# Moving a rotary kernel's later loads and its stores from SyncE's DMA queue to GpSimd's, one packet per engine

## The chip, the cores and the metric

The kernel runs on one core of one Trainium2 chip. The time is device microseconds (us) of one execution; lower is better. Of the core's engines it uses VectorE (DVE) for all arithmetic, and SyncE (SP) and GpSimd (POOL) only to issue transfers, which 16 DMA engines carry out.

## The reference

The input `x` has shape (16, 512, 16, 64): batch, sequence, heads, dimension, in float32, 33.55 MB. `cos` and `sin` have shape (512, 32). Half of each head's 64 values is rotated by a table that depends on the place in the sequence, and the other half is copied through.

```python
x1, x2 = (x[..., :half_dim].copy(), x[..., half_dim:].copy())
rotated_first = x1[..., :half_dim // 2] * cos[..., :half_dim // 2] - x1[..., half_dim // 2:] * sin[..., :half_dim // 2]
rotated_second = x1[..., :half_dim // 2] * sin[..., :half_dim // 2] + x1[..., half_dim // 2:] * cos[..., :half_dim // 2]
return np.concatenate([rotated_first, rotated_second, x2], axis=-1).astype(np.float32)
```

So 33.55 MB must be read and as many written, for about three operations on each value of one half.

## The kernel before

The 8192 rows (batch times sequence) are cut into `T` = 4 tiles. A tile has 128 partitions of `K` = 16 rows, 64 KB in each partition, 8.39 MB in all. On-chip memory holds three of them, the `ring` with `NS` = 3 slots: tile t lies in slot t mod 3, so that tile 3 is loaded over tile 0, once tile 0 has been stored. A tile is rotated in place and then stored whole, the half that is copied through included.

- **Table.** L63 and L64 bring in `cos` and `sin` on POOL's queue (64 KB each), and DVE spreads them over the partitions (L73 to L86).
- **First loads.** L65 to L67 issue on SP's queue the loads of tile 0, of tile 1, and of the first half (`KC` = 8 of 16 rows) of tile 2. None of them waits for anything.
- **Rotation.** `rotate(t, lo, hi)` (L90) is four DVE operations: two products (L96, L97), a difference (L98) and a sum (L101). Each tile takes two calls of half a tile, tile 2 three: rows 0 to 8, 8 to `KM` = 13, and 13 to 16.
- **Behind it on SP's queue**, in this order: the store of tile 0, the load of the second half of tile 2 (which waits for nothing), the load of tile 3 (which waits until the store of tile 0 has landed), the store of tile 1, the store of tile 3.
- **On POOL's queue**: the store of tile 2 (L116), so that it stands in another queue than the store of tile 1.
- **One order by hand**: L118 to L123 make the store of tile 1 wait for `near`, the end of rotating rows 8 to 13 of tile 2, although tile 1 has been ready for longer; the reason given is that it should come behind the loads at the DMA engines.

An engine issues its transfers in program order, and one that waits holds up those behind it on the same engine. Each transfer of 128 partitions is shared by all 16 DMA engines, 8 partitions for each.

Of the kernel before, what the change touches and what calls it, by code (L numbers as in the profile page):

```python
# [1 line left out]

# [4 lines left out]


@with_exitstack
def kernel(  # L10
    ctx: ExitStack,
    tc: tile.TileContext,
    x: bass.AP,
    cos: bass.AP,
    sin: bass.AP,
    out: bass.AP,
):
    nc = tc.nc
    fp32 = mybir.dt.float32
    P = 128  # L20
    B, S, H, D = x.shape
    Q = D // 4
    HF = D // 2

    K = 16
    T = B * S // (P * K)
    PB = S // K
    REP = P // PB  # L30
    R = H * D
    NS = 3
    KC = K // 2
    KM = 13

    xf = x.rearrange("b s h d -> (b s h d)").rearrange("(t p f) -> t p f", t=T, p=P)
    of = out.rearrange("b s h d -> (b s h d)").rearrange("(t p f) -> t p f", t=T, p=P)
    cosf = cos.rearrange("(p k) j -> p (k j)", k=K)
    sinf = sin.rearrange("(p k) j -> p (k j)", k=K)

    const_pool = ctx.enter_context(tc.tile_pool(name="const", bufs=1))
    b_pool = ctx.enter_context(tc.tile_pool(name="bp", bufs=1, space=bass.MemoryType.PSUM))


    ring = const_pool.tile([P, NS, K, H, D], fp32)
    stage = const_pool.tile([P, 2, K, HF], fp32)
    spun = const_pool.tile([P, 2 * K, Q], fp32)
    packed = const_pool.tile([PB, 2 * K, Q], fp32)
    table = const_pool.tile([P, 2, K, 2, Q], fp32)

    def rows(t, lo, hi):
        return ring[:, t % NS, lo:hi].rearrange("p k h d -> p (k h d)")

    def load(t, lo=0, hi=K):
        return nc.sync.dma_start(out=rows(t, lo, hi), in_=xf[t, :, lo * R : hi * R])

    def store(t, lo=0, hi=K, queue=nc.sync):
        return queue.dma_start(out=of[t, :, lo * R : hi * R], in_=rows(t, lo, hi))  # L58


    nc.vector.memset(stage[:, :, :, 0:Q], 0.0)  # L61
    spread = stage.rearrange("(j b) t k i -> j b t (k i)", b=REP)
    nc.gpsimd.dma_start(out=spread[:, 0, 0], in_=cosf)  # L63
    nc.gpsimd.dma_start(out=spread[:, 0, 1], in_=sinf)  # L64
    load(0)  # L65
    load(1)
    load(2, 0, KC)  # L67

    PQ = PB // REP
    nc.vector.stream_shuffle(  # L73
        out=spun[:],
        in_=stage.rearrange("p t k j -> p (t k) j")[:, :, 0:Q],
        mask=[j % PQ * REP for j in range(PB)],
    )
    for q in reversed(range(REP)):
        n = PQ * (q + 1)
        nc.vector.tensor_copy(out=packed[0:n], in_=spun[q * PB : q * PB + n])  # L80

    for r in range(REP):
        nc.vector.tensor_copy(  # L83
            out=table[r * PB : (r + 1) * PB].rearrange("p t k c j -> p (t k) c j"),
            in_=packed.unsqueeze(2).to_broadcast((PB, 2 * K, 2, Q)),
        )  # L86
    C = table[:, 0].rearrange("p k c j -> p k (c j)")
    Sn = table[:, 1].rearrange("p k c j -> p k (c j)")

    def rotate(t, lo, hi):  # L90
        x1 = ring[:, t % NS, lo:hi, :, 0:HF]
        c = C[:, lo:hi].unsqueeze(2).to_broadcast((P, hi - lo, H, HF))
        s = Sn[:, lo:hi].unsqueeze(2).to_broadcast((P, hi - lo, H, HF))
        b_full = b_pool.tile([P, KC, H, HF], fp32, name="b_t")
        b_t = b_full[:, 0 : hi - lo]
        nc.vector.tensor_mul(out=b_t, in0=x1, in1=s)  # L96
        nc.vector.tensor_mul(out=x1, in0=x1, in1=c)  # L97
        nc.vector.tensor_sub(  # L98
            out=x1[:, :, :, 0:Q], in0=x1[:, :, :, 0:Q], in1=b_t[:, :, :, Q:HF]
        )  # L100
        return nc.vector.tensor_add(  # L101
            out=x1[:, :, :, Q:HF], in0=x1[:, :, :, Q:HF], in1=b_t[:, :, :, 0:Q]
        )

    rotate(0, 0, KC)
    rotate(0, KC, K)
    store(0)
    load(2, KC, K)
    load(3)
    rotate(1, 0, KC)  # L110
    rotate(1, KC, K)
    behind_loads = store(1)
    rotate(2, 0, KC)
    near = rotate(2, KC, KM)
    rotate(2, KM, K)
    store(2, queue=nc.gpsimd)  # L116

    tc.add_manual_dep(  # L118
        behind_loads.ins,
        near.ins.name,  # L120
        mybir.DependencyInfo(mybir.DependencyClass.Sync, mybir.DependencyReason.DATA),
        reason="the store follows the loads at the DMA engines",
    )  # L123
    rotate(3, 0, KC)
    rotate(3, KC, K)
    store(3)


# [1 line left out]
_INS = ['x', 'cos', 'sin']  # L130
_OUTS = [((16, 512, 16, 64), 'float32')]


# [23 lines left out]
```

## Time and profile before

| What | Value |
|---|---|
| median of 3 runs | 161.5 us (161.34 to 161.62) |
| span of the profiled execution, first to last instruction | 159.5 us |
| the median less that span (start and end around it) | 2.0 us |
| DVE busy | 112.9 us, its last operation ends at 131.2 us |
| POOL busy | 1.9 us |
| bytes moved | 67.24 MB, 422 GB/s over the span |
| on SP's queue (`q1 hardware_dynamic`) | 58.72 MB in 1152 packets |
| on POOL's queue (`q0 software_dynamic`) | 8.52 MB in 208 packets |

Packets are what the DMA engines are seen to carry out, one after the other. A transfer of a whole tile shows as 128 packets of 64 KB, 8 for each of the 16 engines, and 16 tiny ones that report its end. Transfers are listed with the time from issue to landing, which is when the last of those 16 reports has arrived. When the transfers of a tile are issued and land, from the issues and the times to landing in narrow windows (us from the span's start):

| Transfer | Issued by | Issued | Landed |
|---|---|---|---|
| load, tile 0 | SP | 0.74 | 22.9 |
| load, tile 1 | SP | by 1.3 | 42 |
| load, tile 2, first half | SP | by 1.7 | 52 |
| store, tile 0 | SP | 49.87 | 71.8 |
| load, tile 2, second half | SP | 50.26 | 81.4 |
| load, tile 3 | SP | 71.8 | 100.7 |
| store, tile 1 | SP | 98.86 | 132.1 |
| store, tile 2 | POOL | 104.58 | 144.1 |
| store, tile 3 | SP | 131.2 | 158.6 |

In a table of windows, the bytes and the busy time of a packet are counted where it begins. In a short window the DMA share can so be above 1 or be nothing, though the engines run without a break. In such a table the columns are: window in us, its length, busy us of DVE and of POOL with their instructions, PE clock, DMA share, GB/s.

### The profile page before, as it was taken

To read this page: it belongs to the slowest core of one execution; us is meant where nothing else is said; L and a number is where in the kernel's file an instruction comes from. 1 tells how busy PE (TensorE), PEld (TensorE's weight loads), DVE (VectorE), ACT (ScalarE), POOL (GpSimd) and SP (SyncE) were. 2 spreads that over 40 slices of the span, in tenths; PEclk is the share of its full clock that TensorE was granted. 3 is DMA by queue.
4 is the path that set the end of the run, shared out by engine and by line. 5 is a ranking of instruction groups with operands and counts; after the bars stand their busy time and mean duration, and the time that the engine had idled before them with its cause. 6 is when DMAs were issued, how large, how long until landed. Compare 5 with 4: busy or idle time off the path is not lost.

```text
span 159.5 us, 115 instructions
## 1 busy us (share of the span) xinstructions
DVE 112.9 (71%) x47; POOL 1.9 (1%) x7
## 2 busy tenths in 40 slices
DVE  1000959999999999999999999999999990000000
POOL 3000000000000000000000000010000000000000
DMA  7969979899699699699996996996996996998966
GB/s 263 542 263 542 444 345 526 362 427 526 271 493 551 263 526 526 263 395 427 493 526 263 526 526 263 526 526 263 526 526 263 526 510 279 526 427 362 526 263 263
DMA packets 1360, 67.24 MB, mean 422 GB/s; under 512 B 176, under 2 KB 176, under 8 KB 208
## 3 DMA queue, kind: packets, MB, share of 16 engines
q1 hardware_dynamic: 1152, 58.72, 85.7%
q0 software_dynamic: 208, 8.52, 12.4%
HBM read 33.69 MB, written 33.55 MB: 422 GB/s over the span
## 4 chain that ended last, share of the span: by engine, by line
DVE 61%; DMA 14%; issue 5%; DVEq 1%
DVE b_t L96 22%; DVE ring L97 22%; DMA ring<-in_x_dram 14%; DVE ring L101 10%; DVE ring L98 7%; DVEq L152 1%; DVEq L96 0%
## 5 line engine op out<-in xcount | busy, mean ns | idle before, releaser
L96 DVE TENSOR_TENSOR b_t<-ring,table 128x4096 f32<-128x4096 f32 (+2 forms) x9 | 35.6, 3959 | 2.1 <-DMA ring<-in_x_dram 1.9
L97 DVE TENSOR_TENSOR ring<-ring,table 128x4096 f32<-128x4096 f32 (+2 forms) x9 | 35.6, 3950 | 0.3
L98 DVE TENSOR_TENSOR ring<-ring,b_t 128x2048 f32<-128x2048 f32 (+2 forms) x9 | 18.4, 2050 | 0.3
L101 DVE TENSOR_TENSOR ring<-ring,b_t 128x2048 f32<-128x2048 f32 (+2 forms) x9 | 18.4, 2043 | 0.0
L73 DVE LOAD_MASK_SELECT spun<-stage x1 | 0.0, 14 | 14.4 <-DMA stage<-in_sin_dram 14.4
L83 DVE COPY table<-packed 32x1024 f32<-32x1024 f32 x4 | 2.7, 684 | 0.1
L58 POOL DMA_DIRECT2D out_dram<-ring x1 | 0.6, 559 | 101.7 <-DVE ring L101 101.7
L80 DVE COPY packed<-spun 32x512 f32<-32x512 f32 (+3 forms) x4 | 1.7, 416 | 0.1
L61 DVE MEMSET stage<- 128x512 f32 x1 | 0.5, 485 | 0.9 <-PEq L141 0.9
L73 DVE STREAM_SHUFFLE spun<-stage 128x512 f32<-128x512 f32 x1 | 0.7, 722 | 0.0
L63 POOL DMA_DIRECT2D stage<-in_cos_dram x1 | 0.6, 642 | 1.3 <-DVE stage L61 1.3
L64 POOL DMA_DIRECT2D stage<-in_sin_dram x1 | 0.5, 532 | 0.0
L141 POOL MEMSET const-bfloat16-1.0<- 128x1 bf16 x1 | 0.1, 101 | 0.0
L141 POOL MEMSET const-float32-0.0<- 128x1 f32 x1 | 0.1, 98 | 0.2 <-issue 0.2
L141 POOL MEMSET const-float32-1.0<- 128x1 f32 x1 | 0.1, 98 | 0.0
L141 POOL MEMSET const-uint8-127<- 128x1 uint8 x1 | 0.1, 98 | 0.0
## 6 DMA issues: line engine op xcount, KB each, us to landing
ring<-in_x_dram SPq DMA_DIRECT2D x2, 4096.0 KB, 40.7
stage<-in_cos_dram POOLq DMA_DIRECT2D x1, 64.0 KB, 8.9
stage<-in_sin_dram POOLq DMA_DIRECT2D x1, 64.0 KB, 13.3
ring<-in_x_dram SPq DMA_DIRECT2D x3, 28.9
out_dram<-ring SPq DMA_DIRECT2D x3, 27.4
out_dram<-ring POOLq DMA_DIRECT2D x1, 39.5
```

The source lines that it names most:

```text
L58: return queue.dma_start(out=of[t, :, lo * R : hi * R], in_=rows(t, lo, hi))
L61: nc.vector.memset(stage[:, :, :, 0:Q], 0.0)
L63: nc.gpsimd.dma_start(out=spread[:, 0, 0], in_=cosf)
L64: nc.gpsimd.dma_start(out=spread[:, 0, 1], in_=sinf)
L73: nc.vector.stream_shuffle(out=spun[:], in_=stage.rearrange("p t k j -> p (t k) j")[:, :, 0:Q], mask=[j % PQ * REP for j in range(PB)],)
L80: nc.vector.tensor_copy(out=packed[0:n], in_=spun[q * PB : q * PB + n])
L83: nc.vector.tensor_copy(out=table[r * PB : (r + 1) * PB].rearrange("p t k c j -> p (t k) c j"), in_=packed.unsqueeze(2).to_broadcast((PB, ...
L96: nc.vector.tensor_mul(out=b_t, in0=x1, in1=s)
L97: nc.vector.tensor_mul(out=x1, in0=x1, in1=c)
L98: nc.vector.tensor_sub(out=x1[:, :, :, 0:Q], in0=x1[:, :, :, 0:Q], in1=b_t[:, :, :, Q:HF])
L101: return nc.vector.tensor_add(out=x1[:, :, :, Q:HF], in0=x1[:, :, :, Q:HF], in1=b_t[:, :, :, 0:Q])
L152: with _tile.TileContext(nc) as tc:
```

## The change

```diff
-    def store(t, lo=0, hi=K, queue=nc.sync):
-        return queue.dma_start(out=of[t, :, lo * R : hi * R], in_=rows(t, lo, hi))
+    def reload(t, lo=0, hi=K):
+        return nc.gpsimd.dma_start(
+            out=rows(t, lo, hi), in_=xf[t, :, lo * R : hi * R], single_packet=True
+        )
+
+    def store(t, lo=0, hi=K):
+        return nc.gpsimd.dma_start(
+            out=of[t, :, lo * R : hi * R], in_=rows(t, lo, hi), single_packet=True
+        )
...
-    store(0)
-    load(2, KC, K)
-    load(3)
+    front = store(0)
+    second = reload(2, KC, K)
+    tc.add_manual_dep(
+        second.ins,
+        front.ins.name,
+        mybir.DependencyInfo(mybir.DependencyClass.NoSync, mybir.DependencyReason.DATA),
+        reason="the queue keeps the order of the program",
+    )
+    reload(3)
...
-    store(2, queue=nc.gpsimd)
+    store(2)
```

- The first three loads stay on SP's queue, and `cos` and `sin` on POOL's, as they were.
- The six transfers behind them (store of tile 0, load of the second half of tile 2, load of tile 3, stores of tiles 1, 2 and 3) are all issued by POOL, in this order. SP issues nothing after the first three loads.
- Each of the six is asked for as a single packet: what one DMA engine carries of it (8 rows of 64 KB, or of 32 KB for half a tile) is to be one packet where it was 8.
- The added dependency keeps the load of tile 2's second half behind the store of tile 0 in POOL's program; it is an order, not a wait.
- The waits stay: the load of tile 3 for the landing of tile 0's store, the store of tile 1 for `near`, the stores of tiles 0, 2 and 3 for their last rotation and their load. They are now POOL's.
- DVE's operations and their order are the same.

## The prediction

> **What bounds the kernel now.** I read the totals first, then the transfers with their windows, then what DVE waits for.
>
> ```profile
> span 159.5 us, 115 instructions
> DVE 112.9 (71%) x47; POOL 1.9 (1%) x7
> ...
> HBM read 33.69 MB, written 33.55 MB: 422 GB/s over the span
> ```
>
> DVE, the busiest engine, works 71% of the span and has ended at 131.2 us. The last 28 us are transfers alone. So the question is whether the 16 DMA engines ever rest. In this table of windows, watch how many bytes begin in windows of 0.6 us:
>
> ```profile
> 1.70:2.30 0.60, 0.00 (x0) 0.60 (x1) 1.00 5.30 1748
> 49.80:50.40 0.60, 0.56 (x2) 0.00 (x0) 1.00 2.02 874
> 50.40:51.00 0.60, 0.60 (x1) 0.00 (x0) 1.00 0.00 0
> 51.00:51.60 0.60, 0.60 (x1) 0.00 (x0) 1.00 4.05 1748
> 51.60:53.40 1.80, 1.80 (x1) 0.00 (x0) 1.00 0.00 0
> 53.40:54.00 0.60, 0.60 (x1) 0.00 (x0) 1.00 4.03 1748
> 67.90:68.50 0.60, 0.60 (x1) 0.00 (x0) 1.00 4.62 1748
> ...
> 97.40:98.00 0.60, 0.60 (x2) 0.00 (x0) 1.00 4.03 1748
> 99.80:100.40 0.60, 0.60 (x1) 0.00 (x0) 1.00 4.05 1748
> ```
>
> 1748 GB/s times 0.6 us is 1.05 MB: one packet of 64 KB for each of the 16 engines. The share times the window is its mean time, 4.03 x 0.60 = 2.418 us. The packets begin at 51.0 to 51.6, and the next ones 2.4 us later: back to back. 2.418 us for 64 KB is 27.1 GB/s for an engine and 434 GB/s for 16. One tile is 8 such packets, 19.3 us, and the eight tile transfers (four loads, four stores) are 154.8 us of the 159.5. The rest is 1.7 us before the first packet, a slow first packet (5.30 x 0.60 = 3.18, so 0.76 over), 0.35 where a store is followed by a load (67.9: 4.62 x 0.60 = 2.77), the packets of `cos` and `sin`, and about a microsecond behind the last landing. The kernel is bound by the DMA engines, and the change can only add gaps between packets, or take something off a packet.
>
> **The change part by part.** The span and the 2.0 us around it give the 161.5 us of the median, so what the span gains or loses is added to 161.5.
>
> *The handover at 51 us.* The store of tile 0 is issued when DVE ends its last rotation at 49.85 (L101, 47.57 and 2.28 long). The second row of the table is the last packet of SP's first three loads, 2.02 x 0.60 = 1.21 us long, so the engines run dry between 51.0 and 51.6. The store's packets begin in just that window: SP was in time, with nothing to spare that can be seen. POOL is slower in two steps that the timeline shows:
>
> ```profile
> 0.74 1.33 SPq L55 DMA_DIRECT2D ring<-in_x_dram  x3
> 49.87 0.35 SPq L58 DMA_DIRECT2D out_dram<-ring  x1
> ...
> 103.33 0.95 DVE L101 TENSOR_TENSOR ring<-ring,b_t 128x768 f32<-128x768 f32 x1
> 104.58 0.56 POOL L58 DMA_DIRECT2D out_dram<-ring  x1 [101.70 <-DVE ring L101]
> ```
>
> SP issues 0.02 us behind the DVE operation that it waits for (49.87), and takes 0.35. POOL starts 0.30 behind it (104.58 against 103.33 + 0.95) and takes 0.56. So POOL has the store of tile 0 issued at 49.85 + 0.30 + 0.56 = 50.71, where SP had it at 50.22.
>
> What comes between POOL's issue and the first packet the trace doesn't show, since both times POOL issued here the engines were busy with SP's packets. For SP it can be read: the first load is issued from 0.74 for 0.33 to 0.43 us and its first packets begin from 1.7 on, some 0.6 us after the issue. The lower bound for POOL is nothing; the upper is the tile 2 store, issued at 105.14, whose packets begin at 109.5, 4.4 us later, mostly spent behind SP's packets. Nearest is SP's row. POOL's issue is 1.6 times SP's, so I take 1.6 x 0.6 = 0.95 us. First packets then begin at 51.66, 0.66 us behind 51.0, with the spread that they have now. **Gap: 0.66 us** (0 to 4.1).
>
> The first packet after a rest may be long, as the first of all was: 0.76 over, after 1.7 us without a packet. In proportion to the gap, 0.66 / 1.7 x 0.76 = **0.3 us** (0 to 0.76).
>
> The Trainium skill speaks against the change here: "DMA: Bandwidth & Descriptors", in "Issuing engine by pattern", gives simple loads and stores to SyncE, and its table of specifications puts the first byte at about 1 us on GpSimd's path and 0.6 on SyncE's. By that, as an estimate, POOL's packets would begin at 50.71 + 1.0 = 51.7 or, counted as 0.4 us more than SP's 0.6, at the same 51.7: a gap of 0.7 us. No row here shows POOL's part by itself.
>
> *The second handover, at 100 us.* The store of tile 1 waits for `near`, which ends at 98.83. Its issue on POOL ends at 98.83 + 0.86 = 99.69 and its packets can begin at 100.64. The last packets of tile 3's load begin at 97.4 to 98.0 and end 2.42 later, at 99.8 to 100.4. With SP there was no gap. By itself POOL would leave one of 0.8, but the gap at 51 us moves everything behind it by 0.96, so that the load now ends at 100.8 to 101.4: **nothing is added**. The lateness is paid once, at the first handover.
>
> *The other four.* The second half of tile 2 is issued by POOL right behind the store of tile 0, 19 us before its turn. The load of tile 3 waits for that store to land (71.8, then 72.8), and its issue is covered by tile 2's half, which keeps the engines for 9.7 us. Behind that wait stand the stores of tiles 1, 2 and 3, on POOL now; the first of them is due at 98.8. The stores of tiles 2 and 3 are issued at 105.1 and about 132, while the engines are busy with tiles 1 and 2 until some 139. **Nothing.** If the store of tile 1 were late, all behind it would be, one for one.
>
> *DVE.* It waits for the second half of tile 2 at 90.2 (landed at 81.4) and for tile 3 at 104.3 (landed at 100.7), so that 0.96 later costs it nothing; from 3.6 on, tile 3's rotation would move, and the store behind it has 8 us of cover more. SP, with nothing left to issue, takes no work off the bound.
>
> *One packet where there were eight.* The rows of 64 KB and 32 KB give what a packet costs beyond its bytes: twice 2.02 x 0.60, less 4.03 x 0.60, is 0.006 us. Six transfers lose 7 borders each, 42 x 0.006 = **0.25 us gained** (0 to 0.6 within the rounding of the shares). The row at 67.9, where a store meets a load, could give another 0.35, or stay; I leave it. The skill's same page ("Why small descriptors are slow (HBM only)") puts a fixed cost of some 3 cycles on a packet and holds joining them worthwhile only up to 256 B. By that the gain is no more than the row's, and the packets are 256 times too long for it; as the row is the measurement, it stands.
>
> **Sum:** 161.5 + 0.66 + 0.3 - 0.25 = **162.2 us**.
>
> **The rivals.**
>
> *No gap (faster).* One mechanism: POOL's descriptors reach the engines before 51.0, within 0.3 us of its issue. Then the packets follow each other as now, and the saved borders remain: 161.5 - 0.25 = 161.25, down to 160.9 with all of the borders (0.6), or 160.55 with the 0.35 at the store-to-load border as well. For it: SP's store was in time with no gap to be seen, and POOL's issue ends only 0.49 later. Against: 0.3 us is half of what SP needs. It decides below a gap of 0.25.
>
> *A long start.* 2 to 4.4 us from POOL's issue to the first packet: a gap of 1.7 to 4.1, and up to 0.76 on the packet, 163 to 166.1. For it: `cos`, issued at 2.34, has its packets only at 7.2. Against: these, like those of the tile 2 store, waited behind packets of 64 KB.
>
> *Long packets run worse.* If each single packet starts up as the first load did, 6 x 0.76 = 4.6 us are lost, 166. For it: no packet above 64 KB is in this trace. Against: packets of the tile 2 store, on POOL's queue, take 2.42 as SP's do.
>
> *The change doesn't do what it says:* packets stay 64 KB. Then 161.5 + 0.96 = 162.5.
>
> **How the numbers follow.** Forecast 0.45, no gap 0.35, packets unchanged 0.07, long start 0.08, long packets 0.05. The predicted time is the forecast's 162.2; its own range is 161.6 to 163.0. About 0.2%, 0.3 us, is what a measurement of this kernel can tell from no change. Of "no gap", 0.28 is faster by more than that and 0.07 within it; of the forecast 0.05 is within it and 0.40 slower; unchanged packets give 0.02 and 0.05; the last two are slower. Faster 0.28, same 0.14, slower 0.58. The range goes from 160.9 (no gap, most of the borders saved) to 163.6 (a start of 2 us and a slow first packet); the longer starts, the long packets and the very best case are left out.
>
> **What would show it.** The windows around 51 us show the steps: the first packets of the tile 0 store should begin at 51.6 to 52.3, on POOL's queue, and take more than 2.42 us per 64 KB. At 100 us the packets of tile 1's store should follow the load without a gap. POOL's queue should show some 16 large packets for a tile, with fewer in all. The prediction is wrong if the packets at 51 us leave no gap, if one opens at 100 us as well, or if a tile takes more than 19.4 us in mid-stream.

## The result and the profile after

The changed kernel takes 162.47 us (median of 6 runs, 162.26 to 162.84) where the kernel before takes 161.53 in the same runs: a ratio of 1.0059, 95% interval 1.0049 to 1.0069. It is slower by 0.9 us. The profiled execution has a span of 160.3 us, 0.8 more than before. These are the page's lines on the span, the busy engines and the queues:

```profile
span 160.3 us, 115 instructions
## 1 busy us (share of the span) xinstructions
DVE 112.9 (70%) x47; POOL 4.6 (3%) x12
...
DMA packets 1360, 67.24 MB, mean 419 GB/s; under 512 B 176, under 2 KB 176, under 8 KB 208
## 3 DMA queue, kind: packets, MB, share of 16 engines
q0 software_dynamic: 928, 46.27, 67.3%
q1 hardware_dynamic: 432, 20.97, 30.6%
```

DVE is busy as long as before. POOL's queue now carries 46.27 MB. There are 1360 packets, as many as before: a transfer on POOL's queue still shows as packets of 64 KB or 32 KB.

The windows around the first handover, in the changed kernel (columns as before):

```profile
49.70:50.40 0.70, 0.67 (x2) 0.27 (x1) 1.00 1.73 749
50.40:51.20 0.80, 0.80 (x1) 0.80 (x2) 1.00 0.00 0
51.20:51.60 0.40, 0.40 (x1) 0.01 (x1) 1.00 7.43 2622
...
97.90:98.50 0.60, 0.60 (x1) 0.00 (x0) 1.00 4.03 1748
100.30:100.91 0.61, 0.58 (x2) 0.00 (x0) 1.00 3.98 1719
```

SP's last load packets begin at 49.7 to 50.4 and take 1.21 us, to 51.0 to 51.6. All 16 first packets of the tile 0 store begin between 51.2 and 51.6 (2622 GB/s x 0.40 us is 1.05 MB). So there is hardly a gap, at most 0.3 us on the engines that were done first and next to nothing on the last. But these packets take 7.43 x 0.40 = 2.97 us where 2.42 is usual: **0.55 us over**. They are not long alike. The four that begin last come right behind the load's last packets (which begin at 50.26 to 50.32 and take 1.21), without a rest:

```profile
51.40:51.60 0.20, 0.20 (x1) 0.00 (x0) 1.00 4.30 1311
```

These take 4.30 x 0.20 x 16/4 = 3.44 us, 1.0 over. The other twelve, most of them after a short rest, are 0.4 over in the mean.

At 100 us the store of tile 1 follows the load of tile 3 without a gap and at full pace (3.98 x 0.61 = 2.43).

The issues on POOL, from its timeline:

```profile
50.13 0.56 POOL L63 DMA_DIRECT2D out_dram<-ring  x1 [47.24 <-DVE ring L108]
50.68 0.53 POOL L58 DMA_DIRECT2D ring<-in_x_dram  x1
72.62 0.53 POOL L58 DMA_DIRECT2D ring<-in_x_dram  x1 [21.40 <-DMA out_dram<-ring]
99.10 0.54 POOL L63 DMA_DIRECT2D out_dram<-ring  x1 [25.96 <-DVE ring L108]
104.55 0.54 POOL L63 DMA_DIRECT2D out_dram<-ring  x1 [4.91 <-DVE ring L108]
131.44 0.53 POOL L63 DMA_DIRECT2D out_dram<-ring  x1 [26.35 <-DVE ring L108]
```

The load of tile 3 lands 28.7 us after its issue, at 101.3, against 100.7 before; the last store lands 27.8 us after its issue, at 159.2, against 158.6. So 0.6 us are lost before 101 us, and nothing from there to the last landing. From it to the end of the span are 1.1 us, where before there were 0.9. That is where the 0.8 went: 0.6 at the handover, and 0.2 behind the last landing.

### The profile page after: what moved, and what is told of

Its sections match the earlier page's. It is cut to its first block, busy times and chain, and to the rows that moved or that the text cites. A ratio compares the mean times of both kernels' runs of the same rounds, so it can differ in the third digit from the quotient of the medians.

```text
span 160.3 us, 115 instructions
## 1 busy us (share of the span) xinstructions
DVE 112.9 (70%) x47; POOL 4.6 (3%) x12
## 2 busy tenths in 40 slices
DMA packets 1360, 67.24 MB, mean 419 GB/s; under 512 B 176, under 2 KB 176, under 8 KB 208
## 3 DMA queue, kind: packets, MB, share of 16 engines
q0 software_dynamic: 928, 46.27, 67.3%
## 4 chain that ended last, share of the span: by engine, by line
issue 51%; DVE 15%; DMA 14%; POOL 2%; POOLq 0%; DVEq 0%
DMA ring<-in_x_dram 14%; DVE b_t L103 6%; DVE ring L104 6%; DVE ring L108 3%; DVE ring L105 1%; POOL out_dram L63 1%; POOL ring L58 1%; POOLq L165 0%; POOLq L63 0%; DVEq L103 0%
## 5 line engine op out<-in xcount | busy, mean ns | idle before, releaser
L63 POOL DMA_DIRECT2D out_dram<-ring x4 | 2.2, 541 | 104.5 <-DVE ring L108 104.5
L58 POOL DMA_DIRECT2D ring<-in_x_dram x2 | 1.1, 530 | 21.4 <-DMA out_dram<-ring 21.4
## 6 DMA issues: line engine op xcount, KB each, us to landing
ring<-in_x_dram POOLq DMA_DIRECT2D x1, 28.7
```

Source lines behind the costliest of these rows:

```text
L58: return nc.gpsimd.dma_start(out=rows(t, lo, hi), in_=xf[t, :, lo * R : hi * R], single_packet=True)
L63: return nc.gpsimd.dma_start(out=of[t, :, lo * R : hi * R], in_=rows(t, lo, hi), single_packet=True)
```

## The experiments

Each was timed in turns with the kernel before on one chip; ratios are to that. "Lost" is worked out as above: the mean time of the 16 packets that begin in a window (share x window, x 16 over the packets in it where they are fewer) less 2.42 us, or 1.51 for rows of 40 KB.

**1. The flag.** The changed kernel without `single_packet`, and the kernel before with it on POOL's one store:

```diff
-            out=..., in_=..., single_packet=True
+            out=..., in_=...
```

> The changed kernel without single_packet, all else as changed. Theory (POOL's later start is paid at the handover at 51 us, about 0.6 us, and some 0.2 us come behind the last landing; the flag does nothing): 162.4 us, first packets of the tile 0 store about 3.0 us long as with the flag. Rival (the flag makes the loss, since one long packet starts slowly): 161.5 to 161.7, first packets at 2.42. If the flag saves packet borders as I predicted (0.25): 162.7.

Measured: 162.87 us, 1.0072 (1.0059 to 1.0085), which overlaps the change's interval. Two lines of its profile, which is of the slowest of the five runs (163.47):

```profile
51.40:52.00 0.60, 0.60 (x1) 0.04 (x1) 1.00 4.42 1748
q0 software_dynamic: 928, 46.27, 66.9%
```

The first packets begin at 51.4 to 52.0, a little later than with the flag, and take 4.42 x 0.60 = 2.65. Without the flag nothing is won back, so it doesn't make the loss. The times alone would allow a flag that saves the predicted 0.25, since 162.87 is nearer to the 162.7 which that gives than to 162.4. The packets speak against it: 928 on POOL's queue with the flag and without, so it joined none.

```diff
-    store(2, queue=nc.gpsimd)
+    nc.gpsimd.dma_start(out=of[2], in_=rows(2, 0, K), single_packet=True)
```

> The kernel before with single_packet on the one store that POOL issues (tile 2's), which runs beside tile 1's on SP's queue and there takes turns with it, 64 KB each, and lands 39.5 us after its issue. If the flag makes one packet of what an engine carries: no turns, tile 2's store runs in one piece of 19.3 us and lands some 25 to 30 us after its issue, and tile 1's store later instead. If it does nothing: turns as before, 39.5. Time 161.55 either way.

Measured: 161.58 us, 1.0008 (0.9996 to 1.0019). The store with the flag lands after the same time as before, by the list of issues:

```profile
out_dram<-ring POOLq DMA_DIRECT2D x1, 39.5
```

It still takes turns with tile 1's store. For rows of 64 KB the flag changes nothing that these runs can see.

**2. Only the stores of tiles 1, 2 and 3 on POOL.**

```diff
-    front = store(0)
-    second = reload(2, KC, K)
...
-    reload(3)
+    store_sp(0)
+    load(2, KC, K)
+    load(3)
```

> Store of tile 0, second half of tile 2 and load of tile 3 back on SP's queue as before; the stores of tiles 1, 2 and 3 stay on POOL. Theory with the lateness paid once, at whichever handover comes first: the packets at 51 us as before (2.42 us, no loss), and now a loss of 0.4 to 0.7 us at 100 us, where POOL's issue of tile 1's store ends at 99.6 and the load before it runs out at 99.9 to 100.4; 162.1 to 162.5. Rival (only the handover at 51 us costs): 161.7. Rival (each of the six transfers on POOL costs a like share, 0.15): 161.95, with no loss at 100 us.

Measured: 162.36 us, 1.0049 (1.0037 to 1.0061). (`store_sp` is the old `store` on SP's queue.) The loss has moved from 51 to 100 us, as "paid at the first handover" has it, and the time lies in its 162.1 to 162.5, above both rivals:

```profile
51.00:51.90 0.90, 0.90 (x1) 0.00 (x0) 1.00 2.70 1165
...
97.60:98.10 0.50, 0.50 (x2) 0.00 (x0) 1.00 4.84 2097
98.10:100.50 2.40, 2.37 (x2) 0.56 (x1) 1.00 0.00 0
100.50:100.70 0.20, 0.20 (x1) 0.00 (x0) 1.00 12.69 5243
```

At 51 us, on SP's queue alone, the store's packets take 2.70 x 0.90 = 2.43. At 100 us the load's last packets end at 100.0 to 100.5, POOL's begin at 100.5 to 100.7 and take 12.69 x 0.20 = 2.54: a gap of about 0.3 and 0.12 over. Here POOL really comes late, and what is lost is mostly the gap.

**3. The lateness covered, by more rows ahead.** 10 of tile 2's rows in SP's first load, so that its packets last 2.4 us longer; then also tile 1's store released one row earlier:

```diff
-    load(2, 0, KC)
+    load(2, 0, 10)
...
-    second = reload(2, KC, K)
+    second = reload(2, 10, K)
```

> The changed kernel, with 10 of tile 2's 16 rows in SP's first load instead of 8, so that SP's packets run out 2.4 us later, at 53.4 to 54.0, and POOL's store of tile 0 is waiting by then. Theory (paid once): nothing lost at 51 to 54 us, and 0.4 to 0.7 lost at 100 us, 162.1 to 162.5. Rival (only the first handover costs): 161.7. Rival (a like share for each transfer): 162.4, with no loss at either place.

> As the run with 10 rows ahead, and the store of tile 1 waits for row 12 of tile 2 instead of row 13, so that POOL issues it some 1.7 us earlier, at about 97.4. Both handovers are covered. Theory: no loss at 51 to 54 us and none at 100 us; only what comes behind the last landing is left, 161.6 to 161.8. Rival (a like share for each transfer on POOL): 162.4.

Measured: 162.57 us, 1.0064 (1.0049 to 1.0080), and with `KM = 12` 162.47 us, 1.0058 (1.0046 to 1.0070). The theory's 161.6 to 161.8 for the second fell. The 162.4 of a like share for each transfer is near both times, but experiment 2 spoke against it (161.95 forecast, 162.36 measured), and here too the loss stands in one place. With 10 rows ahead the loss at the first handover is not gone; here the windows of the first of the two runs:

```profile
49.00:49.50 0.50, 0.50 (x1) 0.00 (x0) 1.00 3.03 1311
50.50:51.00 0.50, 0.50 (x1) 0.50 (x2) 1.00 3.78 1311
52.30:53.00 0.70, 0.70 (x1) 0.00 (x0) 1.00 3.05 936
```

SP's load packets of 40 KB take 3.03 x 0.50 = 1.51 us until POOL has issued; the next take 3.78 x 0.50 = 1.89, and the last 3.05 x 0.70 = 2.14 (the 16 of 655 KB). Together 1.0 us is lost while the store stands in its queue behind the load. Being early lost more than being late (1.0 against 0.65). At 100 us, load and store both on POOL's queue, nothing is lost in either run (2.86 x 0.85 = 2.43), not even in the second, where POOL issues the store 1.5 us earlier, at 97.52. This is the second run's line:

```profile
100.25:101.10 0.85, 0.85 (x1) 0.00 (x0) 1.00 2.86 1234
```

**4. The same cover with the six transfers on ScalarE's queue**, a second queue of SP's kind, and without the flag:

```diff
-        return nc.gpsimd.dma_start(
-            out=..., in_=..., single_packet=True
+        return nc.scalar.dma_start(
+            out=..., in_=...
```

> As the run with 10 rows ahead and row 12, with the six transfers on the queue of ScalarE instead of POOL's: also a second queue, but a hardware_dynamic one like SP's. Theory B (two queues, load and store): the same 0.5 to 0.7 lost in the stream, no 0.2 at the end: 162.1 to 162.3. Theory C (POOL's own queue costs it, by how its descriptors are made or fetched): nothing lost, 161.6.

Measured: 162.75 us, 1.0085 (1.0061 to 1.0109), above both theories. Its profile is of the slowest of six runs (163.78; the fastest took 162.42), so its losses are rather upper ends. The load's packets at 50 to 53 us take 2.05 x 0.80 = 1.64 and then 2.36 x 16/15 = 2.52, 1.1 us over. So this loss is not POOL's own. At 98 to 99 us, load and store both on ScalarE's queue, the load's last packets take 2.34 x 1.20 = 2.81, 0.4 over.

**5. Control: 10 rows ahead on SP alone** (the kernel before with the edit of experiment 3 to its loads).

> The kernel before with 10 of tile 2's rows in the first load. Control for the runs with 10 rows ahead, and a try at a faster kernel: in those runs the 0.36 lost where tile 0's store is followed by the load of tile 2's rest was absent. Theory B: nothing lost at 50 to 55 us; if the length of that rest is what matters to the border, 161.2, else 161.55. Rival (10 rows themselves cost the 1.0 at 50 to 55 us): 162.2 or more.

Measured: 162.35 us, 1.0058 (1.0043 to 1.0072). The windows, in a kernel that has load and store on one queue:

```profile
48.70:49.50 0.80, 0.80 (x1) 0.00 (x0) 1.00 1.89 819
50.20:51.00 0.80, 0.80 (x1) 0.00 (x0) 1.00 2.13 819
52.00:53.00 1.00, 1.00 (x1) 0.00 (x0) 1.00 2.56 655
```

1.51, then 1.70 and 2.56: 1.2 us are lost without any second queue, as the rival had it, and theory B's "nothing lost" fell. With 10 rows ahead a second queue adds nothing to the loss. So the runs with 10 rows ahead say nothing on crossing between queues. What they lose at 50 to 55 us belongs to 10 rows, or to a store that stands ready behind the load; these runs don't part the two. Nor is it a faster kernel.

**6. Crossing between queues, at 100 us.** First, POOL's load of tile 3 meets SP's store of tile 1 (the first three transfers of the change on POOL, the rest as before):

```diff
-    behind_loads = store(1)
+    behind_loads = store_sp(1)
...
-    store(3)
+    store_sp(3)
```

> Store of tile 0, second half of tile 2 and load of tile 3 on POOL as in the change; the stores of tiles 1 and 3 back on SP, tile 2's on POOL as before. Theory A (lateness: POOL's packets come late at 51 us): 0.65 lost there, nothing at 100 us, where SP issues tile 1's store at 98.86 in time, and no POOL at the end: 162.2. Theory B (a load on one queue that meets a store on the other costs 0.4 to 1.0, early or late): 0.65 at 51 us and as much again at 100 us, where a load on POOL's queue meets a store on SP's: 162.6 to 163.1.

Measured: 163.54 us, 1.0128 (1.0115 to 1.0142), far above theory A's 162.2, and above theory B's 162.6 to 163.1 too.

```profile
51.20:51.60 0.40, 0.40 (x1) 0.01 (x1) 1.00 7.85 2622
98.10:98.90 0.80, 0.77 (x2) 0.00 (x0) 1.00 3.05 1311
100.50:101.70 1.20, 1.17 (x2) 0.00 (x0) 1.00 2.69 874
```

At 51 us the store's first packets take 7.85 x 0.40 = 3.14 us, 0.7 over. At 100 us, where SP issues the store, 2.69 x 1.20 = 3.23, 0.8 over. The kernel before has 4.05 x 0.60 = 2.43 at that place, and the changed kernel 2.43 as well: nothing lost with both on SP's queue, nor with both on POOL's. The timing isn't quite the same: the load's last packets begin 0.7 to 0.9 us later here than in the kernel before, and the store is issued as early as there, so it stands ready longer. The controls with a store that is issued earlier bound what that is worth: 0 on POOL's queue (experiment 3) and 0.36 on SP's (below). At least 0.4 of the 0.8 is left for the crossing.

The two losses make 1.5 us, and the span is 1.9 longer than before. Most of the rest is at the end: one of the 16 engines begins its last packet about 0.4 us after the others.

Second, experiment 2 with tile 1's store released a row earlier: SP's load meets POOL's store, which now is issued in time.

```diff
-    KM = 13
+    KM = 12
```

> The run with the first three back on SP, and tile 1's store waiting for row 12 of tile 2, so that POOL issues it about 97.7 and SP's load ends at 100. One handover from SP's queue to POOL's, covered. Theory A (lateness): no loss at 100 us, 161.8 with the end's 0.2. Theory B (load on one queue meets store on the other): 0.4 to 1.0 lost between 97 and 102 us, 162.2 to 162.8, and more than the 0.43 of the run in which POOL came late, since the queues overlap longer.

Measured: 163.14 us, 1.0103 (1.0089 to 1.0116), far above theory A's 161.8 and above theory B's 162.2 to 162.8. POOL issues tile 1's store at 97.47, 1.9 us earlier than in experiment 2, and the time gets longer by 0.8 us:

```profile
97.30:97.80 0.50, 0.50 (x1) 0.34 (x1) 1.00 4.93 2097
99.70:100.20 0.50, 0.50 (x1) 0.00 (x0) 1.00 7.57 2097
```

The store's packets begin at 99.7 to 100.2, without a gap, and the first take 7.57 x 0.50 = 3.79 us, 1.4 over. The second run of experiment 3 (with 10 rows ahead besides) has POOL's store at the same place, issued at 97.52, behind a load on POOL's own queue, and loses nothing. The other control is the kernel before with the same `KM`:

> Control: the kernel before with tile 1's store waiting for row 12 instead of row 13; load and store on SP's queue. Theory B: no loss at 100 us, 161.5 to 161.7. Rival (the 1.36 lost at 98 to 102 us in the run with row 12 comes from the earlier issue itself, whatever the queue): 162.6 or more.

Measured: 161.93 us, 1.0025 (1.0017 to 1.0034). On SP's queue the earlier issue costs something too, at the load's last packets:

```profile
97.40:98.00 0.60, 0.60 (x1) 0.00 (x0) 1.00 4.63 1748
```

4.63 x 0.60 = 2.78, 0.36 over: more than theory B's nothing, and far below the 1.4 with two queues. Against this control crossing accounts for some 1.0 us here, in the packets and, less the 0.2 of the end (experiment 8), in the times (163.14 against 161.93).

**7. All tiles through POOL's queue**, `cos` and `sin` through SP's:

```diff
-        return nc.sync.dma_start(out=rows(t, lo, hi), in_=xf[t, :, lo * R : hi * R])
+        return nc.gpsimd.dma_start(out=rows(t, lo, hi), in_=xf[t, :, lo * R : hi * R])
```

> The changed kernel with the first three loads on POOL's queue too, and cos and sin on SP's in their place, so that all tiles go through one queue. POOL's issue of tile 0's store is as late as in the change. Theory A (POOL's lateness at 51 us): 0.55 to 0.65 lost there, 162.2 to 162.4. Theory B (a load on one queue that meets a store on another): no meeting is left; at most the gap of 0.1 seen at 51 us and the 0.15 at the end, 161.7 to 161.9. The start may shift the time by some 0.1 either way.

Measured: 163.98 us, 1.0151 (1.0137 to 1.0164), outside both. The first load's packets begin at 2.6 to 3.4 us, about 1.0 later than before; rotation is late with them, and the store of tile 0 meets engines that have run dry:

```profile
50.50:51.50 1.00, 1.00 (x1) 0.00 (x0) 1.00 1.21 524
51.50:52.90 1.40, 1.36 (x2) 1.03 (x2) 1.00 0.01 0
52.90:53.20 0.30, 0.30 (x1) 0.02 (x1) 1.00 8.39 3495
```

The last load packets end at 51.7 to 52.7, the store's begin at 52.9 to 53.2: a gap of 0.9. But the first packets take 8.39 x 0.30 = 2.52, only 0.1 over. As a test of the time it failed, since it moves the start; the border between tile 0's store and the next load also costs 0.8 here (2.68 x 1.20 = 3.22), where it costs 0.35 in the kernel before. For the packets it tells that a rest of 0.9 us before them doesn't make them long.

**8. The end.** Tile 3's store alone on POOL:

```diff
-    store(3)
+    store(3, queue=nc.gpsimd)
```

> The kernel before with tile 3's store alone on POOL, issued 8 us before its turn. All theories so far put 0.2 us behind the last packet when POOL's queue ends the kernel (1.25 us from the last packet's end to the end of the span before, 1.43 to 1.51 in the five runs with POOL's store last): 161.75 to 161.8, packets as before. Rival (that 0.2 has another cause): 161.6.

Measured: 161.70 us, 1.0013 (1.0004 to 1.0021). The last store lands at 131.64 + 27.1 = 158.7, the span ends at 159.8: 1.0 us where the kernel before has 0.9. The interval begins just above no difference, and holds the 0.2 expected.

## Why the prediction was right, and where it was not

The direction and the place hold: slower by 0.9 us (0.7 forecast), lost at the handover at 51 us; nothing at 100 us; no loss in mid-stream, on DVE or by what waits behind POOL's waits. The sum holds by luck: a gap forecast 0.56 too large stands against a gain of 0.25 that wasn't there, first packets forecast 0.25 too short, and an end of 0.2 left out. Two of its own signs failed: the first packets begin at 51.25 to 51.53, where 51.6 to 52.3 was forecast, and no packet is larger than before. A third, that no gap would prove it wrong, was nearly met.

- **The gap** was mis-sized: 0.66 forecast, 0.1 measured. POOL woke and issued as read from the old trace (0.29 and 0.56 us). From the end of its issue at 50.69 to the first packets, at 51.2 or a little later, are about 0.6 us, just SP's row; stretching it by 1.6 was the larger mistake, 0.4 us. The smaller was to shift all 16 engines alike: only those that were done first had to wait, up to 0.3 us, and the last not at all.
- **The slow first packets** were too small, 0.3 forecast, 0.55 measured, and the reason given was wrong. It was to be a rest before them. In the changed kernel the four packets without a rest are the longest, in experiment 7 a rest of 0.9 us leaves them 0.1 over, and in experiment 6 packets without any rest before them are 0.8 and 1.4 over.
- **What makes them slow** here is the meeting of a load on one queue with a store on the other. Shown at 100 us: 0.8 (POOL to SP) and 1.4 (SP to POOL, row 12), against 0 (SP to SP and POOL to POOL, both with row 13; POOL to POOL with row 12) and 0.36 (SP to SP, row 12); where POOL came 0.3 late (experiment 2) it is 0.1. At 51 us, with the timing as it is, it is 0.55 and 0.7 in the two profiles that cross with the flag on, 0.2 after a short gap without it, and 0 on SP's queue alone. It is no general rule: with 10 rows ahead 1.2 us are lost on SP's queue alone and 1.0 to 1.1 with two queues.
- **The rival "no gap"** came true in its bound, a gap below 0.25, and not in its time; the packets came 0.56 us after POOL's issue and not within its 0.3. It took a covered issue to be free. Experiment 6 shows an issue without a gap that loses more than the late one.
- **The flag's 0.25** was not there: the packets stay as they are, as the rival "packets stay 64 KB" had it. That rival, given a chance of 0.07, had the time too, 162.5, by the same gap and slow packets and so by the same luck.
- **The end** was costed at nothing. By the profiles it is 0.2 in the changed kernel, by experiment 8's time 0.13% or 0.2 us.
- **Paid once** held in the changed kernel, at 100 us. The reason given holds for the gap: POOL's packets could begin at 99.64 + 0.56 = 100.2, and the load, 0.6 later than before, ends only at 100.3 to 100.9; in experiment 2, where it isn't later, there is a gap of 0.3. That the first packets aren't long either has another reason: load and store there are both on POOL's queue, and none is lost there in experiment 3 either, with the store issued later or earlier.

In the trace the sum is 0.1 + 0.55 + 0.2 = 0.85, where the span grew by 0.8 us. The border between tile 0's store and the next load, 2.39 x 1.20 = 2.87 us against 2.77 before, is 0.1 longer and varies from profile to profile by more than that: experiment 2, whose program is that of the kernel before up to there, has 3.27 x 0.90 = 2.94. So differences under some 0.2 us between single profiles say nothing.

Open: why the engines lose time where a load and a store of two queues meet, and why a store ready early behind a load on the same queue costs 0.36 to 1.2 us on SP's and 0.4 on ScalarE's, and nothing on POOL's (experiment 3, at 100 us), and why crossing adds nothing to it with 10 rows ahead. The packets show where the time goes and not what the engines wait for. A store of tile 0 on POOL, ready in time behind SP's load of 8 rows, wasn't tried. No kernel here beats the one before.

## What to carry to other kernels

In a stream that keeps the DMA engines full, look at the places where the direction turns, and try first to leave the load and the store that meet there on one queue: moving a stream to another cost 0.4 to 1.4 us at the crossing here, gaps included, and the most where the issue was in time. With 10 rows ahead it made no difference. An earlier issue is not safer by itself: try it in both directions, with the control that has no second queue. Where the old trace shows an operation only under cover of others, bound its cost with the nearest row as it stands, without scaling it.

## What was not expected

- Two stores on two queues share the engines without loss in the kernel before (tile 2's packets at 109.5 take 4.03 x 0.60 = 2.42); a load and a store lost time, at 51 and at 100 us.
- A store issued 1.5 us earlier on the same queue made the kernel before slower by 0.4 us (experiment 6's control), so its wait for row 13 is worth that much.
- In the runs with 10 rows ahead the store-to-load border, 0.35 over in the kernel before, costs nothing (the run of experiment 5: tile 0's last packets take 2.69 x 0.90 = 2.42), while the border before it costs 1.0 to 1.2.
